# Identity products that lay out S5's input and output, and rotation tables from sines of summed angles

## The chip, the cores and the metric

One NeuronCore of a Trainium2 chip runs the whole program. The metric is the device time of one execution in microseconds. Times are the core's own, from the first to the last instruction and the little that lies around them.

## What is computed

A trunk of two layers over x of 512 tokens by 1024 channels, in fp32. Each layer normalises x, multiplies it by one combined matrix, and splits the result between two mixers. Group A is S5, a diagonal complex state-space model over 32 groups of 16 channels with 64 complex states each, then gelu, a half GLU and an RMS norm. Group B is gated linear attention (GLA) with four heads in chunks of 64 tokens. The two go through one output projection, are added to x, and a SwiGLU FFN follows. Cut to what the change touches:

```python
z = _rmsnorm(x, norm_mix[i]) @ w_in[i]
u_s5, q, k, v, g, gate_lr = split(z)
# S5: s_t = (ar + i ai) s_(t-1) + (bbar u_t);  y = Re(C s_t) + D u_t
y = gelu(_s5_mixer(u_s5, ...))
y = y * sigmoid(y @ s5_w_glu[i] + s5_b_glu[i])
y_s5 = _rmsnorm(y, s5_out_norm[i])
y_gla = silu(g) * groupnorm(gla(q, k, v, gate))
x = x + concatenate([y_s5, y_gla]) @ w_out[i]
x = x + (silu(gate_ffn) * up_ffn) @ w_ffn_out[i]
```

## The kernel before, in words

x is kept transposed: eight tiles `xT` of 128 channels by 512 tokens. Each weight product is an fp32 product in three parts (`mm3`, L620 to L622): high part of the weights by high part of x, high by low, low by high. A dense tile, 128 output channels by 512 tokens, is 24 matmuls of 128x512. The weights come in units of eight 128x128 blocks: a DMA into `raw`, a cast on ACT to `whi` (L163), and a subtraction on DVE, or now and then on POOL, for `wlo` (L165). Two units are looked ahead.

The mixer runs its tiles in one order: `u` 0 to 3 (S5's input), `q`, `k`, `g`, `v`, with the pieces of S5 and GLA between them. The order on TensorE, ACT and the sync engine is the order of the code, and on DVE too in layer 0's mixer up to `region.close()`; on POOL, and on DVE behind that, a scheduler decides.

S5 wants its tokens in another layout than the projection gives: in a tile of `U`, each strip of 32 partitions holds one of four token positions t, for 32 channels, and four such sets of channels j lie side by side. `u_copy` (L782) makes a tile of U out of `us` by 16 ACT copies of 32x128, each from one strip of 32 partitions to another. `s5_fwd` multiplies U by `Wk` (L870); `s5_scan` turns the products by tables `cosT` and `sinT` (L878 to L881 on DVE, L884 and L885 on POOL) and runs eight scans on DVE (L894); `s5_back` turns back (L909 to L918); `s5_y` multiplies the results by `Vx` and U by `Tz` (L932, L934) and takes the gelu out of PSUM in 16 pieces of 32x128 (L943), which undoes the layout. `y_split` makes the high part on ACT (L627) and the low part on DVE (L628) for the GLU `gl`.

The tables of layer 0 are made during layer 0's mixer, step by step, at calls of `bg()`; a tuple `TABLES` says which step is made at which call: "s" small ones, "w" the products for `Wk` (`prep_w_pe`: powers of the state matrix times B, turned by 32-wide products `wt` with the identity on L529, copied out on ACT, L533), "v" `Vx` and `Tz` (`kt` on L553, copies on L566 and L568), "r" the rotation tables. `prep_rot` makes those from fine and coarse angles: seven DVE operations on 128x384 (L582 to L588), three ACT passes on 128x384 (L591 to L593), and then for each of four b six POOL products and sums on 128x512 (L611 to L616). Until b's step, the same columns of `cosT` and `sinT` hold the powers that `wt` reads. Products of this part go to PSUM banks of the pool `aux`, four banks.

Layer 1's tables are made during the FFN of layer 0, on POOL, and its `prep_rot` is not changed.

Of the kernel before, what the change touches and what calls it, by code (L numbers as in the profile page):

```python
# [10 lines left out]
F32 = mybir.dt.float32  # L11
# [5 lines left out]
P = 128  # L17
# [167 lines left out]
def tile_trunk(  # L185
# [41 lines left out]
    def table(name):  # L227
        if loaded[0] != name:
            nc.scalar.preload_act_table_set(name)
            loaded[0] = name  # L230
# [340 lines left out]
    def prep_rot(l, e):  # L571
# [23 lines left out]
        for b in range(NB):  # L595
# [21 lines left out]
            yield  # L617

    def mm3(ps, whi, wlo, xh, xl, start, stop):
        nc.tensor.matmul(ps, whi, xh, start=start, stop=False)  # L620
        nc.tensor.matmul(ps, whi, xl, start=False, stop=False)  # L621
        nc.tensor.matmul(ps, wlo, xh, start=False, stop=stop)  # L622
# [62 lines left out]
    def ntc(t):  # L685
        return t.rearrange("p (n t c) -> p n t c", n=NCH, t=TS)
# [4 lines left out]
    def mix(l, xp, nxt, bg):  # L691
# [43 lines left out]
        def u_pair():  # L735
# [23 lines left out]
            gate_c(1)  # L759
            u_copy(l)  # L760
            if l == 0:
                bg()

        def u_tile(b, mid=None):
            ps = dense(lambda k: ("in", k, b * P), f"u{l}{b}")
            u_scale(b, ps)
            if mid is not None:
                mid()
            u_copy(1 + l)
            if l == 0:  # L770
                bg()

        def u_scale(b, ps):
# [3 lines left out]
        def u_copy(b):  # L777
            u = act(f"U{l}{b}", F32, (P, 4, P))
            pv = ntc(us.pop(b))
            for j in range(4):  # L780
                for t in range(TS):
# [3 lines left out]
                    )  # L785
            U[b] = u

        def r_tile():
# [136 lines left out]
        def s5_y(b):  # L925
# [12 lines left out]
            t_ = y[b] = act(f"y{l}{b}")  # L938
            table(GELU)
            yv = ntc(t_)  # L940
            for j in range(4):
# [193 lines left out]
        def w_s5(n):  # L1135
# [9 lines left out]
            if n >= 1:  # L1145
                while held:
                    s5_evac(*held.pop(0))

        def y_split(b):
            yh[b] = split(f"yg{l}{b}", y[b])  # L1150

        if l > 0:
# [4 lines left out]
            q_tile(0)  # L1157
            s5_back(0)
            s5_fwd(1)
            s5_scan(1)  # L1160
            k_tile(0)
            u_copy(3)
            q_tile(1)
            s5_y(0)
            s5_back(1)
            s5_fwd(2)
            s5_scan(2)
            k_tile(1)
            s5_y(1)
            s5_back(2)  # L1170
            s5_fwd(3)
            s5_scan(3)
            g_tile(0)
            ke_t(0)
            ke_t(1)
            s5_back(3)
            g_tile(1)
            s5_y(2)
# [8 lines left out]
        else:  # L1187
            region.enter_context(tc.manual_schedule(engines={mybir.EngineType.DVE}))
            u_pair()
            u_tile(3, lambda: (gate_b(0), gate_b(1)))  # L1190
            q_tile(0)
            bg()
            k_tile(0)
            bg()
            u_copy(2)
            q_tile(1)
            bg()
            u_copy(3)
            k_tile(1)
            g_tile(0, {4: bg})  # L1200
            bg()
            g_tile(1)
            s5_fwd(0)
            ke_t(0)
            bg()
            s5_scan(0)
            g_tile(2)
            ke_t(1)
            s5_back(0)
            s5_fwd(1)  # L1210
            bg()
            s5_scan(1)
            region.close()

            def s5(b):
# [5 lines left out]
                1: [lambda: s5_back(1), bg],  # L1221
                2: [bg],
                3: [lambda: s5_y(0), lambda: s5(2), bg],
                4: [lambda: score(0), bg],
                5: [lambda: s5_back(2)],
                6: [lambda: s5_y(1), lambda: s5(3)],
                7: [lambda: score(1), lambda: s5_back(3)],
            })
            y_split(0)
            s5_y(2)  # L1230
            y_split(1)
            g_tile(3)
            y_split(2)
            s5_y(3)
            late.append(lambda: y_split(3))

# [164 lines left out]
    with tc.manual_schedule(engines={mybir.EngineType.PE, mybir.EngineType.Activation, mybir.EngineType.SP}):  # L1401
        startup()
        xp = XPrep(0, "nmix")
        small_ = prep_small()
        rots = prep_rot(0, nc.gpsimd)
        nc.gpsimd.memset(Vx, 0.0)
# [19 lines left out]
        for k in range(KD - 3, KD):  # L1426
# [10 lines left out]
        TABLES = (  # L1437
            "s", "", "wssv", "wsr", "wr", "r", "rw", "wv", "wv", "wr", "r", "v", "v", "v", "v",
        )
# [123 lines left out]
```

## Time and profile before

| | us |
|---|---|
| three runs | 1163.48, 1164.62, 1164.71 (median 1164.62) |
| the profiled execution, its own time | 1165.84 |
| its span | 1163.7 |
| mean granted TensorE clock | 0.983 |
| TensorE busy | 1118.5 |
| DVE, ACT, POOL busy | 703.5, 494.7, 320.8 |

The span runs from the first to the last instruction; the execution's own time is a little longer. Layer 0's mixer ends at about 215 us and layer 1's lies between about 610 and 760. In the tables of waits a line names the instruction that stood idle, what released it, the total in us, how often and the longest. A wait for several things is put down to the one that came last. In the windows, "x" counts instructions and PEclk is the granted clock as a share of full speed. Fp32 products are recorded as two matmuls each.

### The profile page before, as it was taken

The numbers are of one execution on the slowest core, as the hardware profiler recorded it, in microseconds if no ns is written. First come the engines' busy times: TensorE is split into PE (matmuls) and PEld (weight loads), VectorE is DVE, ScalarE is ACT, GpSimd is POOL, SyncE is SP. The second block draws the span as 40 slices with busy tenths as digits, with TensorE's granted clock in tenths as the row PEclk, the third lists the DMA queues.
The fourth block names the chain that finished last, engine by engine and source line by source line (L and its number), as shares of the span: only waits on it lengthen the run. The fifth ranks groups of instructions, "written<-read, shape, count | busy, mean of one in ns | idle before, by whom it ended". The sixth has DMA issues, their size and how long they took to land.

```text
span 1163.7 us, 14385 instructions
## 1 busy us (share of the span) xinstructions
PE 1118.5 (96%) x5572; PEld 921.8 (79%) x5572; DVE 703.5 (60%) x919; ACT 494.7 (43%) x856; POOL 320.8 (28%) x310
## 2 busy tenths in 40 slices
PE   8869889999999999999999799999999999999997
PEld 5747677888888888888887688888888888888886
DVE  6898885967554554474464984696544444444454
ACT  6863557453222332432357754745322132222243
POOL 7487853537100043074030350352000000000003
PEclk9979989999999999999999899999999999999999
DMA  6212110233344432233221212123333323233221
GB/s 211 74 51 76 37 55 29 88 125 100 118 109 118 114 105 94 77 110 108 89 83 66 74 55 91 52 90 95 100 100 91 109 92 108 83 99 109 91 91 73
DMA packets 47491, 105.75 MB, mean 91 GB/s; under 512 B 20544, under 2 KB 21696, under 8 KB 47424
## 3 DMA queue, kind: packets, MB, share of 16 engines
q1 hardware_dynamic: 47280, 104.58, 29.3%
q8 instruction: 44, 0.72, 0.3%
q10 hardware_dynamic: 144, 0.26, 0.1%
q14 instruction: 23, 0.19, 0.0%
HBM read 100.63 MB, written 2.10 MB: 88 GB/s over the span
## 4 chain that ended last, share of the span: by engine, by line
PE 82%; DVE 7%; ACT 6%; POOL 2%; issue 1%; DMA 1%; SPq 0%; DVEq 0%; ACTq 0%; POOLq 0%
PE fg L621 7%; PE fg L620 7%; PE fg L622 7%; PE fu L622 7%; PE fu L620 7%; PE fu L621 7%; PE fo L622 7%; PE fo L620 7%; PE fo L621 7%; ACT U L782 2%; DVE ro L894 2%; PE g L620 1%; DVE wlo L165 1%; PE g L622 1%; PE g L621 1%
## 5 line engine op out<-in xcount | busy, mean ns | idle before, releaser
L165 DVE TENSOR_TENSOR wlo<-raw,whi 128x1024 fp32r<-128x1024 f32 x182 | 246.8, 1359 | 131.4 <-ACT whi L163 126.6
L163 ACT CAST whi<-raw 128x1024 fp32r<-128x1024 f32 x183 | 191.6, 1050 | 273.7 <-PE fo L621 111.5
L646 POOL TENSOR_TENSOR sq_fin<-sq_fin 128x512 f32<-128x512 f32 x5 | 6.5, 1294 | 341.8 <-ACT sq_fin L642 341.8
L1295 DVE TENSOR_TENSOR fu<-fu,rs_ffn 128x512 f32<-128x512 f32 x44 | 30.4, 690 | 115.0 <-PE fu L622 112.3
L1312 DVE TENSOR_TENSOR xall<-xall,fo 128x512 f32<-128x512 f32 x78 | 52.9, 685 | 60.3 <-PE fo L622 60.0
L1292 DVE TENSOR_TENSOR fg<-fg,rs_ffn 128x512 f32<-128x512 f32 x44 | 30.2, 687 | 34.1 <-PE fg L622 30.4
L1294 ACT ACTIVATE fg<-fg 128x512 f32<-128x512 f32 x44 | 27.7, 629 | 42.8 <-DVE fg L1292 42.8
L943 ACT ACTIVATE y<-y 32x128 f32<-32x128 f32 x128 | 34.4, 269 | 15.9 <-PE y L934 14.5
L782 ACT COPY U<-us 32x128 f32<-32x128 f32 x128 | 37.8, 295 | 2.5 <-DVE us L775 1.0
L894 DVE TENSOR_TENSOR_SCAN ro<-sp_mag,ro 128x128 f32<-128x128 f32 x64 | 33.1, 581 | 4.6 <-POOL ro L884 4.6
L1296 DVE TENSOR_TENSOR fu<-fg,fu 128x512 f32<-128x512 f32 x44 | 31.9, 725 | 6.0 <-ACT fg L1294 1.3
L1133 POOL TENSOR_TENSOR xall<-xall,wo 128x512 f32<-128x512 f32 x16 | 25.4, 1611 | 24.2 <-DVE wo L1132 24.2
L413 POOL TENSOR_TENSOR pt<-bc,sp_a1r 128x256 f32<-128x256 f32 x2 | 1.2, 623 | 105.4 <-PE fu L622 104.9
L611 POOL TENSOR_TENSOR cosT<-rk 128x512 f32<-128x512 f32 x8 | 11.5, 1438 | 59.9 <-ACT rk L593 56.4
L646 POOL TENSOR_TENSOR sq_x1nmix<-sq_x1nmix 128x512 f32<-128x512 f32 x7 | 9.2, 1319 | 62.0 <-ACT sq_x1nmix L642 62.0
L912 POOL TENSOR_TENSOR sr<-ro,ro 128x508 f32<-128x508 f32 x8 | 14.1, 1762 | 40.6 <-DVE ro L910 40.6
L646 POOL TENSOR_TENSOR sq_s<-sq_s,sq_s 128x512 f32<-128x512 f32 x6 | 8.0, 1340 | 62.4 <-ACT sq_s L642 62.4
L934 PE MATMUL y<-sr,Vx 128*128 128x128 f32 x64 | 14.5, 312 | 7.8 <-POOL sr L912 7.8
L884 POOL TENSOR_TENSOR ro<-ro,ro 128x512 f32<-128x512 f32 x8 | 10.3, 1284 | 28.6 <-DVE ro L880 28.6
L934 PEld LDWEIGHTS y<-sr,Vx 128*128 128x128 f32 x64 | 11.4, 222 | 8.4 <-POOL sr L912 8.4
L418 POOL TENSOR_TENSOR Vx<-pt 64x256 f32<-64x256 f32 x16 | 17.8, 1112 | 0.7
L621 PE MATMUL fg<-x6l,whi 128*128 128x512 f32 x44 | 17.3, 394 | 0.0
(1268 smaller groups left out, 3583.1 us busy)
## 6 DMA issues: line engine op xcount, KB each, us to landing
raw<-in_wst_dram SPq DMA_DIRECT2D x183, 512.0 KB, 3.5
Wk<-wt SPq DMA_DIRECT2D x32, 64.0 KB, 3.9
xall<-in_xt_dram SPq DMA_DIRECT2D x3, 512.0 KB, 8.5
out_dram<-fin SPq DMA_DIRECT2D x6, 256.0 KB, 2.4
bc<-in_s5bc_dram SPq DMA_DIRECT2D x4, 256.0 KB, 4.1
raw<-in_wst_dram SPq DMA_DIRECT2D x1, 384.0 KB, 5.6
cst<-in_const_dram SPq DMA_DIRECT2D x1, 384.0 KB, 4.6
xall<-in_xt_dram SPq DMA_DIRECT2D x1, 275.0 KB, 2.8
```

What stands on the lines that cost most here:

```text
L163: self.nc.scalar.copy(hi, raw)
L165: (self.nc.gpsimd if v in POOL_W else self.nc.vector).tensor_tensor(lo, raw, hi.bitcast(F32), op=ALU.subtract)
L620: nc.tensor.matmul(ps, whi, xh, start=start, stop=False)
L621: nc.tensor.matmul(ps, whi, xl, start=False, stop=False)
L622: nc.tensor.matmul(ps, wlo, xh, start=False, stop=stop)
L782: nc.scalar.copy(u[32 * t:32 * t + 32, j].rearrange("p (n c) -> p n c", n=NCH), pv[32 * j:32 * j + 32, :, t, :],)
L894: nc.vector.tensor_tensor_scan(dst[:, cs], sp["mag4"][:, c:c + 1].to_broadcast([P, P]), src[:, cs], 0.0, M, A)
L943: nc.scalar.activation(yv[32 * j:32 * j + 32, :, t, :], ps[32 * t:32 * t + 32, j * P:(j + 1) * P].rearrange("p (n c) -> p n c", n=NCH), AF ...
L1292: nc.vector.tensor_tensor(g, pg, rstd[0], op=M)
L1295: nc.vector.tensor_tensor(u, pu, rstd[0], op=M)
L1296: nc.vector.tensor_tensor(u, g, u, op=M)
L1312: nc.vector.tensor_tensor(xT[n], xT[n], ps[n], op=A)
```

## The change

Layer 0 alone gets new operations. `u_turn` replaces `u_copy`: for each of four j and four t, a product of 32 columns of the identity with 128 columns of `us` writes one 32-row strip of a PSUM bank of `aux`; one ACT copy of 128x512 moves the bank into U. The gelu of `s5_y` is taken once on 128x512, in S5's layout; `y_turn` then lays the tile out by 16 such products, and the two ACT copies and the DVE subtraction of the split read PSUM. `prep_turn` replaces `prep_rot`: the fine and coarse angles are added first (one DVE operation per b on 128x512), the whole turns taken off (two more), and ACT makes sine and cosine by three passes on 128x512. POOL does nothing of it.

The written order moves too. In layer 0, turns 0 and 1 of u come after u3, 2 after q0, 3 after k0; the `wt` products of b = 2 and 3 stand together before `s5_fwd(0)`, the scores earlier among the tiles of v, and each rotation step at another call of `bg()`. In layer 1 no operation changes, but `s5_fwd(1)` comes after k0 instead of before, `s5_y(0)` and `s5_y(1)` a dense tile later, and so on.

ACT, layer 0, between k's second tile and the second half of the tables for `Wk`. Before (`U` S5's input, `whi` a cast of weights, `wt` the 32-wide products):

```order
L593 ACTIVATE rk_613<-rk_613,bias 128x384
L782 COPY U_673<-us_414 32x128 x16
L163 CAST whi_717<-raw_647 128x1024
L782 COPY U_733<-us_470 32x128 x16
L163 CAST whi_777<-raw_715 128x1024
L533 COPY Wk<-wt_806 128x512
L533 COPY Wk<-wt_824 128x512
L163 CAST whi_853<-raw_775 128x1024
L1040 ACTIVATE g_857<-g_857 128x512
```

After:

```order
L163 CAST whi_738<-raw_670 128x1024
L229 ACT_TABLE_LOAD
L650 ACTIVATE sinT<-cosT 128x512
L651 ACTIVATE cosT<-cosT 128x512
L652 ACTIVATE cosT<-cosT,bias 128x512
L163 CAST whi_781<-raw_736 128x1024
L533 COPY Wk<-wt_803 128x512
L533 COPY Wk<-wt_821 128x512
L650 ACTIVATE sinT<-cosT 128x512
L651 ACTIVATE cosT<-cosT 128x512
L652 ACTIVATE cosT<-cosT,bias 128x512
L163 CAST whi_856<-raw_779 128x1024
```

The two groups of 16 copies are gone from here, and sine passes for b = 0 and b = 1 stand ahead of the weight casts and of the copies out of `wt`.

DVE at the same place. Before (`E`, `Ei`, `Ee` GLA's decays, `qz` its decayed q):

```order
L165 TENSOR_TENSOR wlo_718<-raw_647,whi_717 128x1024
L841 TENSOR_TENSOR E_480<-E_480,rs_mix_343 128x512
L851 SCALAR_TENSOR_TENSOR qz_80<-q_690,E_480 64x4x64 x2
L851 SCALAR_TENSOR_TENSOR qz_81<-q_690,E_480 64x4x64 x2
L165 TENSOR_TENSOR wlo_778<-raw_715,whi_777 128x1024
L860 TENSOR_TENSOR Ei_481<-k_750,Ei_481 128x512
L861 TENSOR_TENSOR Ee_482<-k_750,Ee_482 128x512
L165 TENSOR_TENSOR wlo_854<-raw_775,whi_853 128x1024
L1036 TENSOR_TENSOR g_857<-g_783,rs_mix_343 128x512
```

After:

```order
L165 TENSOR_TENSOR wlo_739<-raw_670,whi_738 128x1024
L893 TENSOR_TENSOR E_463<-E_463,rs_mix_343 128x512
L903 SCALAR_TENSOR_TENSOR qz_80<-q_711,E_463 64x4x64 x2
L903 SCALAR_TENSOR_TENSOR qz_81<-q_711,E_463 64x4x64 x2
L643 TENSOR_TENSOR cosT<-rf_635 128x512
L647 TENSOR_SCALAR sinT<-cosT 128x512
L648 TENSOR_TENSOR cosT<-cosT,sinT 128x512
L165 TENSOR_TENSOR wlo_782<-raw_736,whi_781 128x1024
L912 TENSOR_TENSOR Ei_464<-k_754,Ei_464 128x512
L913 TENSOR_TENSOR Ee_465<-k_754,Ee_465 128x512
L643 TENSOR_TENSOR cosT<-rf_635 128x512
L647 TENSOR_SCALAR sinT<-cosT 128x512
```

Three operations of the table for b = 0 stand between `qz` and the next weight subtraction, and three for b = 1 behind `Ee`.

TensorE in layer 1, around the output products of S5's first quarter. Before (`q`, `k` dense tiles, `y` the output products):

```order
L620 MATMUL q_5322<-x7h,whi_5129 128x512
L621 MATMUL q_5322<-x7l,whi_5129 128x512
L622 MATMUL q_5322<-x7h,wlo_5130 128x512
L932 MATMUL y_5358<-U_5026,Tz 128x128
L934 MATMUL y_5358<-sr_5234,Vx 128x128
L934 MATMUL y_5358<-sm_5235,Vx 128x128
```

After:

```order
L656 MATMUL k_5387<-x7h,whi_5240 128x512
L657 MATMUL k_5387<-x7l,whi_5240 128x512
L658 MATMUL k_5387<-x7h,wlo_5241 128x512
L984 MATMUL y_5420<-U_5043,Tz 128x128
L986 MATMUL y_5420<-sr_5251,Vx 128x128
L986 MATMUL y_5420<-sm_5252,Vx 128x128
```

The same products stand behind the second tile of k where they stood behind the second of q.

The diff:

```diff
--- before.py
+++ after.py
@@ -616,6 +616,42 @@
             e.tensor_tensor(si, si, tw, op=A)
             yield
 
+    def prep_turn(l):
+        sl = slice(16 * l, 16 * l + 16)
+        sh = [P, 16, NROT]
+
+        def v16(t):
+            return t[:, 0:16 * NROT].rearrange("p (a b) -> p a b", a=16)
+
+        cidx = bcast(cidx_t, sh, 1)
+        f, k, g = act(f"rf{l}"), act(f"rk{l}"), act(f"rg{l}")
+        v = nc.vector
+        n = 16 * NROT
+        v.tensor_tensor(v16(f), cidx, bcast(sp["rhi"][:, sl], sh, 2), op=M)
+        v.tensor_scalar(k[:, 0:n], f[:, 0:n], RND, -RND, op0=A, op1=A)
+        v.tensor_tensor(f[:, 0:n], f[:, 0:n], k[:, 0:n], op=SB)
+        v.tensor_tensor(v16(g), cidx, bcast(sp["rlo"][:, sl], sh, 2), op=M)
+        v.tensor_tensor(f[:, 0:n], f[:, 0:n], g[:, 0:n], op=A)
+        v.tensor_scalar(k[:, 0:n], f[:, 0:n], RND, -RND, op0=A, op1=A)
+        v.tensor_tensor(f[:, 0:n], f[:, 0:n], k[:, 0:n], op=SB)
+        yield
+        for b in range(NB):
+            so = slice(4 * b, 4 * b + 4)
+            full = [P, 4, P // 16, 16]
+            co, si = (t[:, so].rearrange("p a b -> p (a b)") for t in (cosT, sinT))
+            t = v16(f)[:, so]
+            v.tensor_tensor(
+                co.rearrange("p (a x y) -> p a x y", a=4, y=16), t[:, :, 16:NROT].unsqueeze(3).to_broadcast(full),
+                t[:, :, 0:16].unsqueeze(2).to_broadcast(full), op=A,
+            )
+            v.tensor_scalar(si, co, RND, -RND, op0=A, op1=A)
+            v.tensor_tensor(co, co, si, op=SB)
+            table(SILU)
+            nc.scalar.activation(si, co, AF.Sin, scale=6.283185)
+            nc.scalar.activation(co, co, AF.Abs)
+            nc.scalar.activation(co, co, AF.Sin, scale=-6.283185, bias=b_hpi)
+            yield
+
     def mm3(ps, whi, wlo, xh, xl, start, stop):
         nc.tensor.matmul(ps, whi, xh, start=start, stop=False)
         nc.tensor.matmul(ps, whi, xl, start=False, stop=False)
@@ -757,18 +793,22 @@
             u_scale(2, ps2)
             gate_c(0)
             gate_c(1)
-            u_copy(l)
             if l == 0:
                 bg()
+            else:
+                u_copy(1)
 
         def u_tile(b, mid=None):
             ps = dense(lambda k: ("in", k, b * P), f"u{l}{b}")
             u_scale(b, ps)
             if mid is not None:
                 mid()
-            u_copy(1 + l)
             if l == 0:
+                u_turn(0)
+                u_turn(1)
                 bg()
+            else:
+                u_copy(2)
 
         def u_scale(b, ps):
             t = us[b] = act(f"us{l}{b}")
@@ -784,6 +824,18 @@
                         pv[32 * j:32 * j + 32, :, t, :],
                     )
             U[b] = u
+
+        def u_turn(b):
+            t_ = us.pop(b)
+            ps = psum(f"ut{l}{b}", "aux")
+            for j in range(4):
+                for t in range(TS):
+                    nc.tensor.matmul(
+                        ps[32 * t:32 * t + 32, j * P:(j + 1) * P].rearrange("p (n c) -> p n c", n=NCH),
+                        C("ident")[:, 32 * j:32 * j + 32], ntc(t_)[:, :, t, :], start=True, stop=True,
+                    )
+            U[b] = act(f"U{l}{b}", F32, (P, 4, P))
+            nc.scalar.copy(U[b].rearrange("p a b -> p (a b)"), ps)
 
         def r_tile():
             psr = R["psr"] = psum(f"r{l}")
@@ -937,6 +989,9 @@
                     )
             t_ = y[b] = act(f"y{l}{b}")
             table(GELU)
+            if l == 0:
+                nc.scalar.activation(t_, ps, AF.Gelu_apprx_tanh)
+                return
             yv = ntc(t_)
             for j in range(4):
                 for t in range(TS):
@@ -1146,6 +1201,23 @@
                 while held:
                     s5_evac(*held.pop(0))
 
+        def y_turn(b):
+            t_ = y[b]
+            ps = psum(f"yt{l}{b}", "aux")
+            for t in range(TS):
+                for j in range(4):
+                    nc.tensor.matmul(
+                        ntc(ps)[32 * j:32 * j + 32, :, t, :], C("ident")[:, 32 * t:32 * t + 32],
+                        t_[:, j * P:(j + 1) * P].rearrange("p (n c) -> p n c", n=NCH), start=True, stop=True,
+                    )
+            hi = act(f"yg{l}{b}h", F32R)
+            nc.scalar.copy(hi, ps)
+            y[b] = act(f"yt{l}{b}")
+            nc.scalar.copy(y[b], ps)
+            lo = act(f"yg{l}{b}l", F32R)
+            nc.vector.tensor_tensor(lo, ps, hi.bitcast(F32), op=SB)
+            yh[b] = (hi, lo)
+
         def y_split(b):
             yh[b] = split(f"yg{l}{b}", y[b])
 
@@ -1156,25 +1228,25 @@
             s5_scan(0)
             q_tile(0)
             s5_back(0)
+            k_tile(0)
+            u_copy(3)
             s5_fwd(1)
             s5_scan(1)
-            k_tile(0)
-            u_copy(3)
             q_tile(1)
+            s5_back(1)
+            k_tile(1)
             s5_y(0)
-            s5_back(1)
             s5_fwd(2)
             s5_scan(2)
-            k_tile(1)
+            g_tile(0)
             s5_y(1)
             s5_back(2)
             s5_fwd(3)
             s5_scan(3)
-            g_tile(0)
             ke_t(0)
             ke_t(1)
+            g_tile(1)
             s5_back(3)
-            g_tile(1)
             s5_y(2)
             g_tile(2)
             y_split(0)
@@ -1189,26 +1261,26 @@
             u_pair()
             u_tile(3, lambda: (gate_b(0), gate_b(1)))
             q_tile(0)
+            u_turn(2)
             bg()
             k_tile(0)
+            u_turn(3)
             bg()
-            u_copy(2)
             q_tile(1)
             bg()
-            u_copy(3)
             k_tile(1)
             g_tile(0, {4: bg})
             bg()
             g_tile(1)
+            bg()
             s5_fwd(0)
             ke_t(0)
-            bg()
             s5_scan(0)
             g_tile(2)
             ke_t(1)
             s5_back(0)
+            bg()
             s5_fwd(1)
-            bg()
             s5_scan(1)
             region.close()
 
@@ -1219,20 +1291,19 @@
             v_tiles({
                 0: [bg],
                 1: [lambda: s5_back(1), bg],
-                2: [bg],
+                2: [lambda: score(0), bg],
                 3: [lambda: s5_y(0), lambda: s5(2), bg],
-                4: [lambda: score(0), bg],
-                5: [lambda: s5_back(2)],
-                6: [lambda: s5_y(1), lambda: s5(3)],
-                7: [lambda: score(1), lambda: s5_back(3)],
+                4: [lambda: s5_back(2)],
+                5: [lambda: score(1)],
+                6: [lambda: y_turn(0), lambda: s5_y(1), lambda: s5(3)],
+                7: [lambda: s5_back(3)],
             })
-            y_split(0)
             s5_y(2)
-            y_split(1)
+            y_turn(1)
             g_tile(3)
-            y_split(2)
+            y_turn(2)
             s5_y(3)
-            late.append(lambda: y_split(3))
+            late.append(lambda: y_turn(3))
 
         upd_a(0)
         upd_b(0)
@@ -1402,7 +1473,7 @@
         startup()
         xp = XPrep(0, "nmix")
         small_ = prep_small()
-        rots = prep_rot(0, nc.gpsimd)
+        rots = prep_turn(0)
         nc.gpsimd.memset(Vx, 0.0)
         nc.gpsimd.memset(Tz, 0.0)
         for t in qz[0] + qz[1]:
@@ -1435,7 +1506,7 @@
         step0 = [0]
 
         TABLES = (
-            "s", "", "wssv", "wsr", "wr", "r", "rw", "wv", "wv", "wr", "r", "v", "v", "v", "v",
+            "s", "", "wssv", "wsr", "w", "r", "wr", "wv", "wwv", "vr", "v", "r", "v", "v",
         )
 
         def bg0():
```

## Rows read from the trace of the kernel before

**Rows 1.** The page, busy time of each engine, share of the span, instructions.
```profile
PE 1118.5 (96%) x5572; PEld 921.8 (79%) x5572; DVE 703.5 (60%) x919; ACT 494.7 (43%) x856; POOL 320.8 (28%) x310
```

**Rows 2.** TensorE's waits, 0 to 260 us: total us, times, longest.
```profile
PE g L622 <- DVE wlo L165: 5.4, 1, 5.4
PE k L620 <- ACT whi L163: 3.3, 1, 3.3
PE sc L1017 <- DVE ro L879: 2.5, 1, 2.5
PE wt L529 <- DVE g L1036: 2.5, 2, 1.9
PE wt L529 <- DVE wk L418: 2.4, 1, 2.4
PE y L932 <- ACT Tz L568: 2.1, 1, 2.1
PE y L934 <- POOL sr L912: 1.6, 1, 1.6
PE y L934 <- POOL sm L918: 1.5, 1, 1.5
...
PE gl L620 <- ACT yg03h L627: 1.5, 1, 1.5
```

**Rows 3.** Windows: us, busy PE, PEld, DVE, ACT, POOL, PEclk, DMA, GB/s.
```profile
59.60:63.00 3.40, 3.10 (x7) 2.48 (x8) 3.29 (x7) 2.44 (x5) 3.19 (x4) 0.51 0.39 154
69.80:76.60 6.80, 4.13 (x10) 3.26 (x11) 6.70 (x10) 5.15 (x16) 4.37 (x5) 0.51 0.28 77
80.05:86.90 6.85, 5.73 (x67) 4.44 (x68) 6.73 (x7) 5.36 (x14) 6.85 (x6) 0.51 0.12 40
110.80:114.20 3.40, 3.40 (x64) 3.03 (x64) 2.62 (x4) 1.59 (x3) 1.50 (x2) 0.51 0.55 159
165.40:172.20 6.80, 5.36 (x36) 5.13 (x40) 6.45 (x6) 1.80 (x5) 4.17 (x3) 0.50 0.18 58
653.50:660.30 6.80, 4.75 (x20) 4.46 (x21) 6.75 (x10) 4.76 (x11) 5.33 (x6) 0.50 0.14 56
```

**Rows 4.** TensorE's waits from 560 us on: total us, times, longest.
```profile
PE y L934 <- POOL sr L912: 6.2, 2, 5.6
PE y L934 <- POOL sm L918: 1.2, 2, 0.7
```

**Rows 5.** TensorE's timeline around g's second tile: start, us, line, operation.
```profile
88.13 0.30 PE L529 MATMUL wt<-cst,bk 128*32 128x128 f32 x1
...
90.02 0.50 PE L620 MATMUL g<-x0h,whi 128*128 128x512 f32 x1
...
95.59 0.38 PE L870 MATMUL x<-U,Wk 128*128 128x128 f32 x2
```

**Rows 6.** TensorE by form, 0 to 260 us: busy us, mean ns.
```profile
L870 PE MATMUL x<-U,Wk 128*128 128x128 f32 x64 | 7.8, 275 | 0.0
```

**Rows 7.** ACT's timeline, 34 to 185 us: start, us, line, operation.
```profile
52.52 4.89 ACT L782 COPY U<-us 32x128 f32<-32x128 f32 x16
...
83.44 1.05 ACT L163 CAST whi<-raw 128x1024 fp32r<-128x1024 f32 x1
...
99.71 0.59 ACT L533 COPY Wk<-wt 128x512 f32<-128x512 f32 x1
...
134.93 4.48 ACT L943 ACTIVATE y<-y 32x128 f32<-32x128 f32 x16
```

**Rows 8.** DVE's timeline, both layers' mixers: start, us, line, operation.
```profile
83.08 1.53 DVE L165 TENSOR_TENSOR wlo<-raw,whi 128x1024 fp32r<-128x1024 f32 x1
...
86.11 1.73 DVE L851 SCALAR_TENSOR_TENSOR qz<-q,E 64x256 f32<-64x256 f32 x4
...
98.43 0.68 DVE L878 TENSOR_TENSOR ro<-x,cosT 128x512 f32<-128x512 f32 x1
...
662.65 2.62 DVE L894 TENSOR_TENSOR_SCAN ro<-sp_mag,ro 128x128 f32<-128x128 f32 x8
```

## The prediction

> **What bounds the kernel now.** First the page's busy time by engine: TensorE is busy for 96% of the span [rows 1], so a gain must come out of the remaining 4%, out of work taken off TensorE (the change takes none off; it adds some) or out of stretches in which TensorE's clock was granted at half. Second, TensorE's waits in the first 260 us [rows 2]: nine lines of that table, of 1.5 us and more, belong to layer 0's mixer behind 50 us, and they wait for three different engines. Third, the granted clock in the stretches where it fell [rows 3]: about 0.5, the 1.2 GHz level, in five pieces of layer 0's mixer and one of layer 1's, each next to one of those waits; the rows elsewhere stand at full clock. In them TensorE was busy 3.10 + 4.13 + 5.73 + 3.40 + 5.36 us in layer 0 and 4.75 in layer 1; at full clock that work takes half as long, so the low clock cost 10.9 and 2.4 us. Fourth, the same waits from 560 us on [rows 4]: 6.2 + 1.2 us, all before S5's output products of layer 1. The FFNs are not touched by the change. So what can move is these waits and six slow stretches: about 23 + 11 us in layer 0 and 7.4 + 2.4 us in layer 1.
>
> **The change, term by term.** Every term is in the time of the one profiled execution, 1165.84 us.
>
> *The price of a turn.* A turn is 16 products, 32 columns of identity by 128 columns of data, in fp32. The nearest row is `wt`: 32 products of that form, recorded as 64, start at 88.13 and the next tile starts at 90.02 [rows 5], so 16 take 0.95 us. The four neighbours write different 32-row strips of PSUM, as the turn's do, and evidently ran side by side. The dense tile behind them took 5.57 us until the next group at 95.59 [rows 5]. To 0.95 I add 0.2 for entering and leaving such a group twice as often: 1.15, an estimate. From the other side, 128-wide fp32 products: 32 of them, recorded as 64, took 7.8 us [rows 6], so 16 take 3.9 us if nothing runs side by side. I take 1.15, since the row of the same shape says so; 3.9 stays for the slower rival. Less than nothing is excluded: the products are new work on the busiest engine. Eight turns cost 9.2 us, four before 65 us and four in the second half.
>
> *What ACT loses.* Sixteen copies per u tile took 4.89 us, sixteen gelus per y tile 4.48 [rows 7]. In their place stand one copy of 128x512, and for y one gelu and two copies, of 0.59 each by the nearest copy out of PSUM [rows 7]. For k's second tile this is the whole cause: its weight cast stood behind the copy at 52.52. In the new order the copies that stand ahead of that cast are 0.59 each. So the 3.3 us before k [rows 2] go, and nothing takes their place there: the line names ACT, not the DMA that feeds the cast.
>
> *Layer 0 up to v (term A).* Removed: waits of 5.4 + 3.3 + 2.5 + 2.4 = 13.6 us [rows 2], and half of 3.10 + 4.13 + 5.73 + 3.40, 8.2 us [rows 3]. Put in their place:
> (1) Before g's first tile DVE still does seven angle operations and a subtraction. They start some 4.9 us earlier, by the U copy; TensorE gets there only 0.3 earlier (3.3 of wait and 1.6 of half clock gone, four turns of 4.6 added). 5.4 - 4.9 + 0.3 leaves about 1.0 us.
> (2) The products for Wk wait for DVE's power operations. DVE is 4.9 us earlier, TensorE by then 6.7 (4.4 from g, 0.3, and 2 of half clock): 2.4 + 1.8 = 4.2 us.
> (3) A new wait, before g's second tile. Its PSUM bank comes free when ACT copies out the first `wt` tile; the order shows three sine passes and a weight cast ahead of that copy on ACT, and the sine waits for three new DVE operations, which stand behind wlo, E and qz. Counted from the end of the powers: wlo, E and two qz are 4.8 us beside a busy POOL (83.08 to 86.11 + 1.73) [rows 8], of which I take 4.2; the three DVE operations are 2.0 at 0.68 each and 4.6 at 1.5 (E's pace between those rows) [rows 8], I take 3.2, since POOL still makes the powers; three passes on ACT at 0.59, the cast at 1.05, one copy at 0.59 [rows 7] make 3.4. Together 10.8. TensorE has 1.0 of `wt`, nine of 24 matmuls of g's tile (2.05) and 1.9 of the next `wt`: 5.0. The wait is 6 us; 3.5 to 8 with the ends.
> (4) 1.0 us of small waits for PSUM drains, and half clock behind the waits of (2) and (3): two stretches at the mean loss of the four before, 4.1.
> (5) Four turns, 4.6, and `kt`, which comes into this stretch out of the next: 64 records like `wt`, 1.9.
> A = -13.6 - 8.2 + 1.0 + 4.2 + 6.0 + 1.0 + 4.1 + 4.6 + 1.9 = +1.0 us. The gain up to v is eaten.
>
> The Trainium skill, SBUF — State Buffer, section Who interferes with whom, says that a DVE operation with two inputs in SBUF contends with a GpSimd operation that reads SBUF, and that one blocks the other; by it all the turn's DVE operations would go at the 1.5 us pace, (3) would be 1.4 us longer and the whole 1.4 later. The rows agree on the size (0.68 and about 1.5), not on how often POOL will be reading.
>
> *Layer 0 from v on (term B).* POOL no longer does the 24 products and sums of the rotation tables; its queue holds only the powers for Vx and S5's own operations. Waits that hung on it or on DVE behind it: sc 2.5, Tz 2.1, sr 1.6, sm 1.5 [rows 2]. I let all go, 7.7: `kt` and with it Tz come 8 us earlier, s5_back and scans no longer share with rotation work, and y's tiles 1 and 2 stand later. Half of 5.36 [rows 3] goes with sr and sm: 2.7. `kt` leaves: 1.9. Three y turns come in: 3.45. B = -8.85.
>
> *The GLU's start (term C).* Its wait of 1.5 for the last y split [rows 2] goes, one turn (1.15) comes. The chain behind the last y (gelu, copies, subtraction, some 2.5 us) is hidden by `up` and the three other k-blocks of the GLU; without that cover it would cost 1.9 more. C = -0.35.
>
> *Layer 1 (term D).* Only the written order changes. Before, y0 stands right behind q1; now k1 is between, a dense tile of 5.57 [rows 5] against the wait of 5.6 [rows 4]. But DVE sets the pace here: each S5 step is eight operations of 0.68 and eight scans of 2.62 [rows 8], 8.1 us, beside weight subtractions, and now k1 comes earlier and waits for its own. All gone is -7.4 - 2.4 = -9.8; a mere shift is 0. I take -4, a little under the middle, because the same DVE queue feeds y1.
>
> **Sum:** +1.0 - 8.85 - 0.35 - 4.0 = -12.2; 1165.84 - 12.2 = 1153.6. The profiled execution is 1.2 over the median of the runs, 1164.62, so the forecast is 1152.4.
>
> **The rivals.**
> *The ring of DVE and ACT is longer.* Turn, sines, cast, copy and PSUM bank follow each other for b = 0, 1 and again for 2 and 3 amid the scans; at the long end of (3), 8 us, twice, and with Tz's copies behind sines, layer 0 gains nothing: only -4 is left, 1160.6. For it: (3) is a chain with no slack in the order. Against: the second pair of tables is wanted late.
> *The products run one after another: slower.* At 3.9 us a turn, eight cost 31.2 instead of 9.2, 22 more: 1174. It decides from 2.7 us a turn on (1.15 + 12.2/8). For it: the data in the turn is read with a stride, where `wt` reads the identity. Against: 64 records of the same shape in 1.89 us.
> *Contention ends with POOL's rotations.* Then (3) is at 3.5, half clock comes once, and layer 1 gives 7: 2.5 + 2.0 + 3.0 and some 1 from scans, 8.5 better, 1144.
> *Layer 1's wait only moves* to k1 and y1: D is 0, 1156.4.
> *The change doesn't do what it says:* were rotations still on POOL, B would lose half. POOL's order is 24 rows shorter, so I give it nothing.
>
> **How the numbers follow.** Forecast 0.55 (1148 to 1157 with the ends of (1) to (3) and D from -7 to -1), layer 1 only moves 0.10, longer ring 0.15, contention ends 0.12, serial products 0.08. The range takes in all but the last and the outer ends: 1143.5 to 1161. A difference of 0.2%, 2.3 us, is about what a measurement of this kernel can tell from no change. Faster gets the forecast, the moved wait, the end of contention and 0.08 of the ring (its 1160.6 is 0.35% faster): 0.85; same the other 0.07 of the ring, which takes layer 1's gain too; slower 0.08, the serial products.
>
> **What would show it.** Right: no wait of k for whi; turns of about 1.1 us; a wait of some 6 us for ACT's Wk copy before g's second tile; v starting within 2 us of 114; no wait over 1 us from v to the GLU; full clock from 165 to 172; y0 of layer 1 without its 5.6 us. Wrong: turns of over 2.7 us, waits in front of y for sr that stayed, v starting after 120, or layer 1's waits standing under another name with the same sum.

## The result: 5 us faster, where 12 were forecast

The changed kernel takes 1159.5 us (median of five runs, 1157.7 to 1159.98) against 1164.62 for the kernel before (1163.48 to 1165.05): a ratio of 0.9948, 95% interval 0.9936 to 0.996. It is faster, as forecast, and inside the range, but the gain is 5.1 us where the forecast had 12.2. The profiled execution's span is 1158.0 us against 1163.7.

The busy time of the changed kernel, from its page, to be held against [rows 1]:

```profile
PE 1121.7 (97%) x5828; PEld 923.9 (80%) x5828; DVE 697.8 (60%) x931; ACT 471.2 (41%) x749; POOL 290.9 (25%) x286
```

Work went where the diff says: 24 us left ACT, 30 left POOL. TensorE gained 256 recorded matmuls, the eight turns. Then three instants on TensorE, which cut the execution into pieces: the first matmul of the output projection of layer 0 (`wo0s`, the end of what the mixer waits for), the first u matmul of layer 1 and the first matmul of layer 1's output projection (`wo1s`). TensorE's timeline, start and duration, the kernel before:

```profile
194.11 0.48 PE L620 MATMUL wo0s<-so00h,whi 128*128 128x512 f32 x1
...
601.98 0.39 PE L620 MATMUL u<-x0h,whi 128*128 128x512 f32 x1
...
746.69 0.48 PE L620 MATMUL wo1s<-so10h,whi 128*128 128x512 f32 x1
```

and the changed kernel:

```profile
185.37 0.48 PE L656 MATMUL wo0s<-so00h,whi 128*128 128x512 f32 x1
...
593.22 0.39 PE L656 MATMUL u<-x0h,whi 128*128 128x512 f32 x1
...
740.90 0.48 PE L656 MATMUL wo1s<-so10h,whi 128*128 128x512 f32 x1
```

Layer 0's mixer ends 8.74 us sooner. The output projection and the FFN between take 407.9 us in both. Layer 1's mixer, whose first u matmul stands at 602 us in the kernel before and not at about 610, takes 740.90 - 593.22 = 147.7 us where it took 144.7: it lost 3.0. The rest of the program takes 417 us in both. The forecast had given layer 0 8.2 us and layer 1 4.0. So the missing 7 us are all in layer 1, in which the change only moved instructions.

The table of TensorE's waits of the changed kernel up to 260 us, those of layer 0's mixer, which answers to [rows 2] (columns as there):

```profile
PE g L656 <- ACT Wk L533: 5.4, 1, 5.4
PE g L658 <- DVE wlo L165: 2.9, 1, 2.9
PE x L922 <- DVE sc L1081: 2.3, 1, 2.3
...
PE wt L529 <- ACT Wk L533: 1.4, 1, 1.4
PE wt L529 <- DVE g L1091: 1.3, 1, 1.3
...
PE wt L529 <- DVE wk L423: 0.5, 1, 0.5
```

k's wait for its weights, both waits of y for POOL and the one of the GLU are gone. The first line is the new ring that the forecast had named (turn, sines, cast, copy, PSUM bank), the third one it had not. From 560 us on, against [rows 4]:

```profile
PE kT L1034 <- ACT y L998: 3.1, 1, 3.1
PE y L986 <- POOL sr L964: 2.6, 1, 2.6
PE k L656 <- ACT whi L163: 1.2, 1, 1.2
PE y L986 <- POOL sm L970: 1.0, 2, 0.7
PE k L658 <- DVE wlo L165: 0.9, 1, 0.9
```

The 6.2 us for sr became 2.6, but two waits of k and one of `kT` stand beside it: 8.8 us where 7.4 stood. Windows of the changed kernel at low clock, to be read like [rows 3]:

```profile
86.00:94.00 8.00, 8.00 (x50) 6.32 (x54) 4.84 (x8) 3.23 (x5) 0.00 (x0) 0.77 0.22 66
131.00:139.00 8.00, 8.00 (x37) 6.53 (x38) 7.13 (x12) 0.19 (x1) 3.47 (x4) 0.80 0.19 66
673.00:681.00 8.00, 8.00 (x32) 6.52 (x32) 6.72 (x14) 1.36 (x3) 4.57 (x6) 0.79 0.00 0
```

The first two stand behind the waits of 5.4 and 2.3 us, the last behind that of `kT` (3.1) in layer 1. A window of 8 us at 0.77 lost about 1.8 us against full clock.

### The profile page after: what moved, and what is told of

Read it like the earlier page. It is cut to its first block, busy times and chain, and to the rows that moved or that the text cites. A ratio compares the mean times of both kernels' runs of the same rounds, so it can differ in the third digit from the quotient of the medians.

```text
span 1158.0 us, 14789 instructions
## 1 busy us (share of the span) xinstructions
PE 1121.7 (97%) x5828; PEld 923.9 (80%) x5828; DVE 697.8 (60%) x931; ACT 471.2 (41%) x749; POOL 290.9 (25%) x286
## 4 chain that ended last, share of the span: by engine, by line
PE 83%; DVE 10%; ACT 4%; issue 1%; DMA 1%; POOL 0%; SPq 0%; DVEq 0%; ACTq 0%
PE fg L657 7%; PE fg L656 7%; PE fg L658 7%; PE fu L658 7%; PE fu L656 7%; PE fu L657 7%; PE fo L657 7%; PE fo L658 7%; PE fo L656 7%; DVE wlo L165 2%; DVE ro L946 1%; PE v L1012 1%; PE v L1013 1%; PE v L1014 1%; PE g L656 1%
## 5 line engine op out<-in xcount | busy, mean ns | idle before, releaser
L165 DVE TENSOR_TENSOR wlo<-raw,whi 128x1024 fp32r<-128x1024 f32 x182 | 242.5, 1335 | 127.7 <-ACT whi L163 126.2
L946 DVE TENSOR_TENSOR_SCAN ro<-sp_mag,ro 128x128 f32<-128x128 f32 x64 | 28.0, 499 | 5.4 <-POOL ro L936 5.4
L936 POOL TENSOR_TENSOR ro<-ro,ro 128x512 f32<-128x512 f32 x8 | 10.3, 1284 | 52.9 <-DVE ro L932 52.9
L611 POOL TENSOR_TENSOR cosT<-rk 128x512 f32<-128x512 f32 x4 | 6.6, 1660 | 54.2 <-ACT rk L593 54.2
L822 ACT COPY U<-us 32x128 f32<-32x128 f32 x64 | 18.9, 296 | 1.7 <-DVE us L815 1.0
L922 PE MATMUL x<-U,Wk 128*128 128x128 f32 x128 | 16.8, 286 | 2.4 <-DVE sc L1081 2.3
L998 ACT ACTIVATE y<-y 32x128 f32<-32x128 f32 x64 | 17.2, 269 | 3.6 <-PE y L986 2.9
L922 PEld LDWEIGHTS x<-U,Wk 128*128 128x128 f32 x128 | 15.8, 199 | 3.2 <-issue 2.5
L656 PE MATMUL fg<-x0h,whi 128*128 128x512 f32 x44 | 17.2, 392 | 0.0
```

What stands on the lines that cost most here:

```text
L165: (self.nc.gpsimd if v in POOL_W else self.nc.vector).tensor_tensor(lo, raw, hi.bitcast(F32), op=ALU.subtract)
L922: nc.tensor.matmul(ps[part][:, j * P:(j + 1) * P], Wk[:, part, 4 * b + j], U[b][:, j], start=True, stop=True,)
L946: nc.vector.tensor_tensor_scan(dst[:, cs], sp["mag4"][:, c:c + 1].to_broadcast([P, P]), src[:, cs], 0.0, M, A)
```

## Where layer 1 lost: the order, and kT above all

**Theory.** `s5_y(1)` now stands after g's first tile, and the two `kT` transposes still follow right behind S5's last products. Each takes a PSUM bank of the pool `aux` of four. In the written order y1, two tiles of S5's products and the first `kT` take the four banks, so the second `kT` gets that of y1, which ACT empties in 16 pieces. TensorE's rows of the changed kernel in layer 1:

```profile
667.00 1.95 PE L922 MATMUL x<-U,Wk 128*128 128x128 f32 x16
668.78 0.60 PE L1034 MATMUL kT<-cst,Ee 128*128 128x128 f32 x4
672.45 0.66 PE L1034 MATMUL kT<-cst,Ee 128*128 128x128 f32 x4 [3.06 <-ACT y L998]
```

and ACT's at that place:

```profile
667.93 4.47 ACT L998 ACTIVATE y<-y 32x128 f32<-32x128 f32 x16
672.42 0.59 ACT L1036 COPY keT<-kT 128x512 f32<-128x512 f32 x1
```

y1's last product ended at 667.2, its gelu at 672.4, and the second `kT` began at 672.45. In the kernel before, g's first tile (5.6 us) lay between y1 and `kT` and covered the gelu. Its rows, ACT's and TensorE's:

```profile
672.61 4.48 ACT L943 ACTIVATE y<-y 32x128 f32<-32x128 f32 x16 [3.73 <-PE y L934]
...
679.68 1.03 PE L979 MATMUL kT<-cst,Ee 128*128 128x128 f32 x8
```

The rival: layer 1 is slower because of what it inherits from a layer 0 that ends sooner.

### Layer 1's order taken back (e1)

```diff
             s5_back(0)
-            k_tile(0)
-            u_copy(3)
             s5_fwd(1)
             s5_scan(1)
+            k_tile(0)
+            u_copy(3)
             q_tile(1)
-            s5_back(1)
-            k_tile(1)
             s5_y(0)
+            s5_back(1)
             s5_fwd(2)
             s5_scan(2)
-            g_tile(0)
+            k_tile(1)
             s5_y(1)
             s5_back(2)
             s5_fwd(3)
             s5_scan(3)
+            g_tile(0)
             ke_t(0)
             ke_t(1)
-            g_tile(1)
             s5_back(3)
+            g_tile(1)
```

> The changed kernel with layer 1's mixer written in the order of the kernel before; layer 0 as changed. Theory one, the new order of layer 1 costs 3.0 us (its mixer, from the first u matmul to wo1s, took 147.7 us against 144.7 before): 1159.5 - 3.0 = 1156.5, and layer 1's waits are again y0's 5.6 and some 1.8. Rival, layer 1 is slower because of what it inherits from a shifted layer 0 (weight units, DVE's backlog), not by its order: no change, 1159.5 within 1 us.

Measured: 1156.93 us, ratio to before 0.9925 (0.9911 to 0.9938). The kernel before was timed again beside each group of runs (1166.03 us here), and the ratios go by that. Span 1154.9, 3.1 less than the changed kernel's. `wo0s` starts at 185.39, layer 1's mixer takes 144.7 us. The old waits are back, and `kT` waits for nothing:

```profile
PE y L986 <- POOL sr L964: 6.5, 2, 5.6
```

### The order alone on the kernel before (e2)

The same lines, the other way, in the kernel before.

> The kernel before with nothing changed but the written order of layer 1's mixer. Theory one: 3.0 us slower, 1164.6 + 3.0 = 1167.6, with a wait of about 3 us of kT for ACT's gelu of y1. Rival (inherited state): as before, 1164.6 within 1 us. The forecast had said 4 us faster, 1160.6.

Measured: 1167.24 us where the kernel before took 1166.03 in the same series, ratio 1.0013 (1.0004 to 1.0021). The trace says more than the time: layer 1's mixer went from 144.7 to 147.6 us. In this execution layer 0, which is untouched, ended at 195.57 instead of 194.11, so single executions of one program differ there by some 1.5 us. The timed loss, 0.5 to 2.4 us by the interval, is smaller than the trace's 2.9; the trace is of the longest of the eleven executions (1169.83), and why the times show less stays open. Waits from 560 us on:

```profile
PE kT L979 <- ACT y L943: 3.3, 1, 3.3
PE y L934 <- POOL sr L912: 2.7, 1, 2.7
PE k L620 <- ACT whi L163: 1.2, 1, 1.2
```

With layer 0 as it was, the same waits appear. The other traces say the same: with the new order layer 1's mixer took 147.6 to 147.7 us in the changed kernel, e2, e5, e6, e7 and e9, whether layer 0 ended at 176.6 or at 195.6, and with the old one 144.7 in the kernel before, e1 and e12. Only e4, with the new order, differs (146.1, its `kT` waits 2.2 us), for a reason that is open. So it is the order and nothing inherited: the rival falls.

### kT behind g's second tile (e3)

```diff
             s5_scan(3)
-            ke_t(0)
-            ke_t(1)
             g_tile(1)
+            ke_t(0)
+            ke_t(1)
             s5_back(3)
```

> The changed kernel, layer 1's two kT transposes moved behind g's second tile, nothing else. Theory: the second kT waits for the PSUM bank that the gelu of y1 (16 pieces, 4.5 us) holds, and the new order has no dense tile between the two; with g's tile between them the 3.1 us go and g's tile runs at full clock (1.6): 1155 to 1156. Rival: DVE sets the pace of the whole stretch, so the wait only moves to y2 or g2: within 1 us of 1159.5.

Measured: 1154.71 us, ratio 0.9903 (0.989 to 0.9917); span 1153.0, layer 1's mixer 142.7 us. That is 5.0 less than with `kT` ahead: the wait's 3.1 and the half clock behind it. It is also 2.0 less than in the kernel before, so the new order is worth something once `kT` has cover. The longest waits that stay:

```profile
PE y L986 <- POOL sr L964: 2.6, 1, 2.6
PE k L656 <- ACT whi L163: 1.2, 1, 1.2
```

### DVE relieved in layer 1 (e8)

On top of e3, one weight subtraction went from DVE to POOL (`POOL_W = (17, 101)`).

> The kernel with kT behind g's second tile in layer 1 (e3, 1154.7), and one more change: the weight subtraction of the unit that g's second tile of layer 1 uses is made by POOL, not by DVE. Theory: DVE's queue sets the pace of layer 1's mixer, so 1.2 us less of it before y1 gives 1.2 us and some half clock, 1152.5 to 1153.5. Rival: POOL's 2.4 us operation slows DVE as much as it relieves it, or sr waits behind it: 1154.5 to 1156.

Measured: 1155.27 us, ratio 0.9905 (0.9891 to 0.9919), the same as e3. Layer 1's mixer took 143.3 us against 142.7. The wait of y for sr went from 2.6 to 2.4. The rival's number held. What limits the rest of layer 1's mixer is not settled by it: DVE is busy for 45.4 of the 50 us from 630 to 680 in the changed kernel, but one subtraction less there bought nothing.

## What the three parts of layer 0's change did

### Rotations back on POOL (e4)

```diff
-        rots = prep_turn(0)
+        rots = prep_rot(0, nc.gpsimd)
...
-            "s", "", "wssv", "wsr", "w", "r", "wr", "wv", "wwv", "vr", "v", "r", "v", "v",
+            "s", "", "wssv", "wsr", "wr", "r", "wr", "wv", "wwv", "vr", "v", "r", "v", "v",
```

> The changed kernel with layer 0's rotation tables again from 24 products and sums on POOL, all else as changed. By the forecast (POOL's rotations were behind the waits for sr, sm, sc and slowed DVE's scans) about half of the 8.7 us that layer 0's mixer gained is lost: 1163.5 to 1164.5. Rival, the gain is the layout's and the order's, and POOL has room: 1159.5 within 1 us; with no sines ahead of the Wk copies on ACT the 5.4 us wait before g's second tile may even go, 1156.

Measured: 1160.18 us, ratio 0.9958 (0.9946 to 0.9971), as the changed kernel within the intervals. In the trace `wo0s` starts at 187.43, 2.1 us later, and the loss lies ahead of v: v starts at 114.60 instead of 112.23, and from there to the first `up` matmul it is 51.8 us against 52.1. The wait before g's second tile did go, but another came:

```profile
PE x L922 <- DVE g L1091: 6.7, 1, 6.7
...
PE wt L529 <- DVE g L1091: 2.5, 1, 2.5
```

The 6.7 us go back to POOL. Rotation products and powers for `Vx` stand ahead of POOL's two sums for S5's first scans (the first is L936), DVE's scans wait for these, and the drain of g's tile, which TensorE waits for, stands behind the scans on DVE:

```profile
102.69 1.06 POOL L614 TENSOR_TENSOR sinT<-rg,rk 128x512 f32<-128x512 f32 x1
...
105.32 1.26 POOL L936 TENSOR_TENSOR ro<-ro,ro 128x512 f32<-128x512 f32 x1
...
106.61 4.49 DVE L946 TENSOR_TENSOR_SCAN ro<-sp_mag,ro 128x128 f32<-128x128 f32 x8 [8.30 <-POOL ro L936]
```

So the 2.1 us are a net: this wait came, and the ring's waits of 5.4 and 1.4 went. They are not what taking the rotations off POOL is worth; e9 below, with the sines on ACT and no ring, ends layer 0 10.8 us sooner than e4. What e4 does refute is the forecast's reason for term B: POOL still made rotation products from 116 to 139 us, and none of the four waits of that term came back.

### U by copies (e5), and its opposite (e12)

e5 puts the 64 ACT copies of layer 0 back at their old places (the lines for the first two tiles of u are left out here):

```diff
             q_tile(0)
-            u_turn(2)
             bg()
             k_tile(0)
-            u_turn(3)
             bg()
+            u_copy(2)
             q_tile(1)
             bg()
+            u_copy(3)
             k_tile(1)
```

> The changed kernel with layer 0's u laid out again by 64 ACT copies at their old places, no u products. By the forecast's steps the four u products cost 4.2 us of TensorE, against 3.3 + 1.6 us of wait and half clock before k and a DVE that runs 4.9 us later: with the copies back layer 0 is 3 to 5 us longer, 1162.5 to 1164.5. Rival: the products only trade places with the wait (what they save before k they cost as work), 1159.5 within 1 us.

Measured: 1165.83 us, ratio 1.0003 (0.9993 to 1.0012): all the gain is gone, more than expected. `wo0s` starts at 193.03, 7.7 us later than in the changed kernel, and v starts 7.7 us later too (119.93).

```profile
PE g L656 <- ACT Wk L533: 9.1, 1, 9.1
PE g L658 <- DVE wlo L165: 6.0, 1, 6.0
PE k L656 <- ACT whi L163: 3.4, 1, 3.4
```

The 3.4 and the 6.0 are the old waits. The 9.1 is the ring of sines with a U copy in it. ACT's timeline of e5:

```profile
86.44 0.72 ACT L652 ACTIVATE cosT<-cosT,bias 128x512 f32<-128x512 f32 x1
87.07 4.87 ACT L818 COPY U<-us 32x128 f32<-32x128 f32 x16
91.97 1.04 ACT L163 CAST whi<-raw 128x1024 fp32r<-128x1024 f32 x1
92.92 1.07 ACT L533 COPY Wk<-wt 128x512 f32<-128x512 f32 x2
```

e12 is the kernel before with only the u products, at the places of the changed kernel:

> The kernel before with one part of the change alone: u of layer 0 laid out by products, at the places of the changed kernel; sines, y and orders as before. From e5 (the changed kernel without this part, 7.7 us longer in layer 0): 4 to 8 us faster than before, 1157 to 1161. By the forecast's steps: four products cost 4.2, k's wait gives 4.9 back and g's and wt's stay about as they are, so 0 to 2 us faster, 1163 to 1166.

Measured: 1162.12 us against 1167.32 in its series, ratio 0.9961 (0.9949 to 0.9974), 3 to 6 us faster. In the trace `wo0s` starts at 190.66, 3.5 us sooner. In time that is about what the whole change brings, but the whole loses 3.0 us in layer 1; in layer 0 it is 3.5 of 8.7. The forecast's steps had it at 0 to 2: they let k's wait go, but held those of g and `wt` as they were. g's wait for wlo fell too, from 5.4 to 2.9, while the waits of `wt` for DVE's g grew from 2.5 to 5.2.

### y in pieces (e6)

The gelu again in 16 pieces per tile, and `y_split` at its old places, behind v and around g's fourth tile, instead of `y_turn`.

> The changed kernel with layer 0's gelu again in 16 pieces per tile and the split of y on ACT and DVE, no y products. The four y products cost 4.3 us of TensorE. By the forecast's terms they buy the 1.5 us before the GLU and some of the waits in front of y (their banks come free 4 us sooner): without them 1159 to 1162. Rival: ACT has room from v on and the pieces are hidden behind dense tiles, the products are pure cost: 1155.5 to 1157.

Measured: 1161.94 us, ratio 0.9958 (0.9942 to 0.9974); the runs scatter from 1157.61 to 1163.68, so the time does not tell it from the changed kernel. The trace is of one of the longer executions (1163.57); three of the eight took 1157.61 to 1159.17, no longer than the changed kernel. In the trace `wo0s` starts at 189.31, 3.9 us later: from v to `up` 2.8 us less, from `up` on 6.4 more, with a wait in front of the GLU

```profile
PE gl L656 <- ACT yg03h L663: 3.3, 1, 3.3
```

In that execution the four products of 1.1 us stand against a chain on ACT that TensorE waited for; that they pay in every execution is not shown. The undone parts cost 2.1, 7.7 and 3.9 us in the traces, 13.7 in sum, more than the 8.7 that the whole gained: the parts do not add up one by one.

## The ring before g's second tile

DVE's rows of the changed kernel, the chain as the forecast had written it down (E and qz are left out between the first and the second row):

```profile
75.26 1.65 DVE L165 TENSOR_TENSOR wlo<-raw,whi 128x1024 fp32r<-128x1024 f32 x1
...
79.83 0.69 DVE L643 TENSOR_TENSOR cosT<-rf 128x512 f32<-128x512 f32 x1
80.56 0.73 DVE L647 TENSOR_SCALAR sinT<-cosT 128x512 f32<-128x512 f32 x1
81.32 0.99 DVE L648 TENSOR_TENSOR cosT<-cosT,sinT 128x512 f32<-128x512 f32 x1
```

ACT's:

```profile
82.34 0.63 ACT L650 ACTIVATE sinT<-cosT 128x512 f32<-128x512 f32 x1 [13.02 <-DVE cosT L648]
...
84.30 1.03 ACT L163 CAST whi<-raw 128x1024 fp32r<-128x1024 f32 x1
85.23 1.06 ACT L533 COPY Wk<-wt 128x512 f32<-128x512 f32 x2
```

and TensorE's:

```profile
85.86 0.79 PE L656 MATMUL g<-x0h,whi 128*128 128x512 f32 x1 [5.35 <-ACT Wk L533]
```

From 75.26 to 85.86 it is 10.6 us, forecast 10.8. Is it worth taking away?

### The first two sines one call later (e7)

```diff
-            "s", "", "wssv", "wsr", "w", "r", "wr", "wv", "wwv", "vr", "v", "r", "v", "v",
+            "s", "", "wssv", "wsr", "w", "", "wr", "wrv", "wwv", "vr", "v", "r", "v", "v",
```

> The changed kernel with the rotation steps of b = 0 and 1 one call later, so that on ACT the Wk copies of b = 0 stand ahead of all sines. Theory: the 5.4 us before g's second tile are the ring of three DVE operations, three sines, a cast and the copy, and go, with the half clock behind them (1.9): 1152.5 to 1155. Rival: DVE and the drains set the pace there, and the wait stands again before the next wt, s5's first products or g's third tile: 1158 to 1160.

Measured: 1157.88 us, ratio 0.9931 (0.9919 to 0.9944); `wo0s` at 184.52, 0.9 us sooner, which is no more than executions of one layer 0 differ (e8, whose layer 0 is the changed kernel's, has 184.57). The wait moved to the third `wt`, as the rival said:

```profile
PE wt L529 <- ACT Wk L533: 4.3, 1, 4.3
```

The copies for b = 1 now stood behind the sines of b = 0.

### The sines behind all copies (e9)

```diff
-            "s", "", "wssv", "wsr", "w", "r", "wr", "wv", "wwv", "vr", "v", "r", "v", "v",
+            "s", "", "wssv", "wsr", "w", "", "w", "wv", "wwrrv", "vr", "v", "r", "v", "v",
```

> The changed kernel with the rotation steps of b = 0 and 1 behind all products for Wk, so that no Wk copy stands behind a sine. In e7 the wait before g's second tile went and 4.3 us stood before the third wt in its place, since the copies of b = 1 stood behind the sines of b = 0. Theory: with the sines last both go, only DVE's drains of g (1.3 to 1.9 us) stay: layer 0's mixer ends 5 to 7 us sooner, 1152.5 to 1154.5. Rival: the tables then come too late for the scans, and y of the first quarter or the scores wait: 1157 to 1159.5.

Measured: 1149.72 us, ratio 0.9852 (0.9837 to 0.9867); `wo0s` at 176.60, 8.8 us sooner than in the changed kernel, more than expected. No line names `Wk` any more; the longest waits are now:

```profile
PE g L658 <- DVE wlo L165: 2.8, 1, 2.8
PE x L922 <- DVE sc L1081: 2.5, 1, 2.5
PE wt L529 <- DVE wk L418: 1.7, 1, 1.7
```

The waits for Wk, 5.4 and 1.4, make 6.8 us; the half clock behind the first some 1.8. The tables were still in time: ACT's sines ran from 91.28 to 95.3 and y of the first quarter did not wait.

### Both layers (e10), and later U copies (e11)

e10 is e9 with e3's `kT` and the first scores two k-blocks of v later (`2: [bg]`, `4: [score(0), s5_back(2)]`).

> e9, kT behind g's second tile in layer 1 as in e3, and in layer 0 the first scores two k-blocks of v later, where the old order had them, so that S5's products do not wait 2.3 us for DVE's masks. Theory: the three gains add up, -5 to -7, -4.8 and -2.3 us against 1159.5: 1146 to 1148.5. Rival: layer 0's pieces share DVE and only two of three count: 1149 to 1151.

Measured: 1146.55 us, ratio 0.9828 (0.9814 to 0.9841), the fastest kernel of this study: some 13 us under the changed kernel's 1159.5, 20.8 under the kernel before that was timed beside it (1167.32). `wo0s` at 175.96, layer 1's mixer 143.5 us. The third gain did not come: S5's products still wait 2.9 us for the masks of the scores, only at another place (137.88 us). That the time fell into the range of the three gains all the same is owed to the first, which was 8.8 us where 5 to 7 were expected.

e11 writes layer 1's third and fourth U copies behind q's and k's second tile.

> e10 with layer 1's third and fourth U copies (4.9 us of ACT each) written behind q's and k's second tile. Theory: the 1.2 + 0.9 us before k's second tile are a weight cast behind these copies, and go: 2 us less than e10. Rival: DVE is the pace of layer 1, and y0 or y1 wait by as much more: within 0.7 us of e10; if S5's third products then wait for their U copy, 1 to 2 us slower than e10.

Measured: 1147.45 us, ratio 0.9833 (0.982 to 0.9847), no difference from e10 within the intervals. The 2.1 us before k went; 1.2 before g, 0.8 before `kT` and 0.6 before y came in their place, and layer 1's mixer took 144.2 us against 143.5. The rival held in the trace (0.7 us); the medians differ by 0.9.

## Why the prediction went wrong, step by step

- **Price of a turn:** right. The two turns behind u3 lie between 38.73 and 40.62, 0.95 us each, the single ones take 1.0 to 1.1; forecast 1.15. The products run side by side, and the rival of serial products is out.
- **Term A, up to v:** v starts at 112.23 instead of 114.23, with `kt` already done: -2.0 us, forecast +1.0. The parts were off in both directions: g's wait for wlo 2.9 (1.0), the powers 0.5 (4.2), the ring 5.4 (6.0), the drains and the copies between the `wt` 2.7 (1.0). These four make 11.5 us against 12.2; the turns took 3.9 for 4.6, the half clock behind the waits of 2.9 and 5.4 some 3.7 for 4.1, and the remaining 1.2 us were not taken apart. The largest miss, the powers, came from leaving DVE's power operations as long as they were: they took 5.6 us (69.67 to 75.2), where 73.65 to 83.05 were 9.4 in the kernel before.
- **The rule of the Trainium skill** (SBUF — State Buffer, Who interferes with whom), worked out in the forecast, would have put the turn's three DVE operations at 1.5 us each. They took 0.69, 0.73 and 0.99 us, although POOL was busy for all of the 2.6 us from 79.80; the same three for b = 1, with POOL idle, took 0.68, 0.43 and 0.69. So the loss was 0.6 us in sum. POOL's third product there took 1.12 us where the two before it took 0.62, so POOL may have been the one that was held; these rows do not decide whether one blocks the other, as the Trainium skill says.
- **Term B, from v on:** from the start of v to `up` 52.1 us instead of 57.2: -5.1, forecast -8.85. All four waits went. What the term had not, a new wait: S5's third products take a bank of the scores, which were moved ahead of them, and wait 2.3 us for DVE's masks; 1.6 us of half clock follow. And its reason that POOL no longer makes the rotations does not hold: with them back on POOL the same stretch took 51.8 us (e4), with the u copies back 52.1 (e5), with y in pieces 49.3 (e6), but 57.5 in e12, which has the old order. That leaves the written order, with `kt`'s earlier place in it, as what took the waits away; no run changes layer 0's order alone, so this is argued and not shown.
- **Term C:** -1.7, forecast -0.35. The chain behind y no longer makes the GLU wait; that the y products pay for themselves is shown for one execution of e6 only.
- Terms A to C together: -8.7, forecast -8.2. That the sum came out is luck: A gained 3.0 us and C 1.3 more than forecast, B 3.8 less.
- **Term D, layer 1:** this is the step that failed. The forecast gave -4, between the two ends "all gone", -9.8, and "a mere shift", 0. It came out at +3.0, outside both ends. The step weighed the waits that the order removes and named DVE as the pace, but followed no other piece that was moved: it never asked what stands between y1 and the next user of y1's bank. The rows for it were there: a gelu of 4.48 us [rows 7], and behind y1 only S5's products and one transpose. e1 and e2 show the order as the cause, and e3 that `kT` makes 5.0 us of it: without `kT` term D would have been -2.0, inside the ends.
- **The rivals:** "layer 1's wait only moves" (1156.4) came nearest in kind, but ended at 0 where the order lost. The longer ring (1160.6) gave the time nearest to the measured one for a reason that did not occur: the ring was as long as forecast.

## What to carry to other kernels

Where an order is rewritten, follow every PSUM bank from its last reader to its next writer, and look for a dense tile between them; a wait for a bank of a small ring does not show in the table of waits of the old kernel. Look also at what stands ahead of copies that set banks free: here, moved behind the last of them, the same sines made no wait. And when one term's two bounds have the same sign, say what would have to happen for the other sign.

## What was not expected of the hardware

A wait cost more than its length. Behind the 5.35 us wait the granted clock stood at 0.77 over the next 8 us (0.50, the 1.2 GHz level, from 86 to 88 us), and taking away 6.8 us of waits shortened layer 0 by 8.8. And executions of the same instructions in layer 0 ended up to 1.5 us apart (194.11 and 195.57; 185.37 and 184.57), so a difference of a us between two traces shows no effect.
